# Other places for weights and tokens in SBUF, and another order of three products, in a pool/SSD/ConvFFN layer

## The chip, the core and the metric

The kernel runs on one core of a Trainium2 chip. The metric is the device time of one execution in microseconds, as the median of several runs. Beside it stands one profiled execution, whose trace holds every instruction with its start and length.

The engines of the core appear under these names: PE (TensorE, matrix products), PEld (its loads of weights), DVE (VectorE), ACT (ScalarE), POOL (GpSimd) and SP (SyncE, which here only issues DMAs). SBUF is the on-chip memory of 128 partitions; an address below is a byte offset inside a partition. PSUM holds the sums of matrix products.

## The reference

One layer for two request groups that share the weights: 256 tokens of a new stream and 32 tokens of a running one, so 288 tokens of 2048 numbers, all in float32.

```
proj = rmsnorm(x) @ w_in          # 2048 -> u_pool 1024 | z 2048 | xBC 2560 | dt 32
pool = pool_mixer(u_pool)         # trailing means over 2/4/8/16 tokens, then w_pool
ssd  = ssd_mixer(z, xBC, dt)      # causal conv, Mamba-2 scan, gate, grouped rmsnorm
x    = x + rmsnorm(concat[pool, ssd] @ w_out)      # 3072 -> 2048
up   = causal_dwconv(rmsnorm(x) @ w_up)            # 2048 -> 2 x 5632
x    = x + rmsnorm((silu(gate) * val) @ w_down)    # 5632 -> 2048
```

It also returns new states of the pool, the convolutions and the scan. Nearly all arithmetic lies in four products: w_in, w_out, w_up and w_down.

## The kernel before

**Products in two parts.** A float32 number is split in a high part (rounded to the type float32r, in which a matmul streams) and a low part, what is left of it. A product of weights and tokens is then three matmuls into one PSUM sum: high weights by high tokens (L146), high weights by low tokens (L147), low weights by high tokens (L148). Function `mm3` issues these three. Weights are the stationary operand, 128 x 128, loaded anew for each matmul (as many PEld as PE instructions); tokens are the moving operand, 288 columns. A group of three such matmuls, for 128 rows of K (a K-tile) and 128 output columns, is called a triple below.

**Projections.** Function `project` computes one group of output columns, mostly 256 (two PSUM sums of 128): it goes over K in chunks (`ksplit`), fetches each chunk of weights with one DMA on SP's queue into a raw tile (`fetch_w`), splits it in parts of up to 1024 elements a partition, ACT writing the high weights and DVE the low ones (`split_w`, L140 and L141), and issues the triples: for each part, for each of the two sums, for each of the part's K-tiles. A part is four K-tiles of 256 columns. There are 82 such groups: 19 of w_in, 6 of w_out, 42 of w_up, 15 of w_down (in two halves of K, with w_up's second half between). The last two output tiles of w_down are written out by hand at the end of the kernel (L1268, L1269 and L1291), as are the first chunks of w_in at its start (L364). The pool's products (`pool_group`) use `mm3` too.

**Order.** A scheduler that simulates the program orders the instructions of the engines; `tc.high_priority` brings weight fetches and splits ahead, and `pin` fixes the order of some instructions.

**Places in SBUF.** Tiles come from pools, which lie one behind another in a partition in the order in which they are opened; a tile's size is rounded up to 32 bytes. The order is: `const`, `whi` (high weights), `side1`, `wlo` (low weights), `wraw` (raw weights), `apool` (tokens: xn, mixs, hn, each with high and low halves of 288 numbers, 1152 bytes apart), `bpool`, and then the pools of single stages. Weight and token buffers are multiples of 256 bytes long, and so are a K-tile's rows and, at 512 bytes, the two column blocks of a weight tile. All high weights therefore start at one address modulo 256, all low weights at another, and all high tokens at a third. `side1` holds one tile, `rec`, of 64 bytes, so that low weights stand 64 bytes behind the high weights, modulo 256; the tokens, too, stand 64 bytes behind the high weights. `FC_GAP` gives the activations of the feed-forward stage (fa) the same place as the tokens of `apool`; the pool's outputs in the w_out stage (mixp) stand 128 bytes off it. In the first stage high and low weights are the two halves of one tile, 3072 bytes apart. wlast (the last weights of the tail) lies in raw buffers, which before the change have the tokens' place modulo 256.

Of the kernel before, what the change touches and what calls it, by code (L numbers as in the profile page):

```python
# [8 lines left out]
F32 = mybir.dt.float32  # L9
# [7 lines left out]
P = 128  # L17
# [8 lines left out]
HEADS = 32  # L26
# [3 lines left out]
NX = D_SSD // P  # L30
# [22 lines left out]
TURN_AT = 13  # L53
FC_GAP = 48
NEAR = 8


@with_exitstack
def body(
# [23 lines left out]
    act, dve, pool, pe, sp = nc.scalar, nc.vector, nc.gpsimd, nc.tensor, nc.sync  # L83

    const = ctx.enter_context(tc.tile_pool(name="const", bufs=1))
    wpool = {"hi": ctx.enter_context(tc.tile_pool(name="whi", bufs=4))}
    side1 = ctx.enter_context(tc.tile_pool(name="side1", bufs=1))
    wpool["lo"] = ctx.enter_context(tc.tile_pool(name="wlo", bufs=4))
    wpool["raw"] = ctx.enter_context(tc.tile_pool(name="wraw", bufs=4))
    apool = ctx.enter_context(tc.tile_pool(name="apool", bufs=16))  # L90
    bpool = ctx.enter_context(tc.tile_pool(name="bpool", bufs=20))
    acc_ps = ctx.enter_context(tc.tile_pool(name="acc_ps", bufs=5, space=PSUM))
# [6 lines left out]
    def atile(name):  # L99
        return apool.tile([P, 2, NT], F32R, tag="a", name=name)  # L100

    def btile(name):
        return bpool.tile([P, NT], F32, tag="b", name=name)
# [17 lines left out]
    def fetch_w(view, kb, nk, c0, nc_):  # L121
        raw = wpool["raw"].tile([P, nk, nc_], F32, tag="raw", name="raw")
        with tc.high_priority(offset=ahead[0]):
            group, c = divmod(c0, 2 * P)
            sp.dma_start(out=raw, in_=view[group, :, kb : kb + nk, c : c + nc_])
        return raw

    def split_w(raw, kb, nk, nc_, after=()):

        out = []  # L130
        step = min(nk, 1024 // nc_)
        for k in range(0, nk, step):
            n = min(step, nk - k)
            hi = wpool["hi"].tile([P, n, nc_], F32R, tag="hi", name="whi")
            lo = wpool["lo"].tile([P, n, nc_], F32R, tag="lo", name="wlo")
            with ExitStack() as order:
                order.enter_context(tc.high_priority(offset=ahead[0]))
                for ins in after:
                    order.enter_context(tc.issue_after(ins.ins))
                act.activation(hi, raw[:, k : k + n, :], AF.Copy)  # L140
                dve.tensor_tensor(lo, raw[:, k : k + n, :], hi.bitcast(F32), op=ALU.subtract)  # L141
            out.append([(kb + k + i, hi[:, i, :], lo[:, i, :]) for i in range(n)])
        return out

    def mm3(out, wh, wl, a, start, stop, then=lambda ins: ins):
        then(pe.matmul(out, wh, a[:, 0, :], start=start, stop=False))  # L146
        then(pe.matmul(out, wh, a[:, 1, :], start=False, stop=False))  # L147
        then(pe.matmul(out, wl, a[:, 0, :], start=False, stop=stop))  # L148

    def project(view, groups, acts, ksplit, before=None, done=None, spare=(), hold=(), behind=None, wait=(), tail=()):  # L150


        n_all = sum(-(-w // P) for _, w in groups)
        accs = [acc_ps.tile([P, NT], F32, tag="acc", name="acc") for m in range(n_all - len(spare))]
        accs.extend(spare)
        k_first, k_last = ksplit[0][0], ksplit[-1][0] + ksplit[-1][1] - 1
        after = before(*ksplit[0]) if before else None
        for i, (kb, n) in enumerate(ksplit):
            raws = [fetch_w(view, kb, n, c0, w) for c0, w in groups]
            nxt = None  # L160
            if before and i + 1 < len(ksplit):
                nxt = before(*ksplit[i + 1])
            m0 = 0
            for raw, (c0, w) in zip(raws, groups):
                parts = split_w(raw, kb, n, w, tuple(wait) + ((after or ()) if m0 else ()) + (hold if i else tail if m0 + w // P == n_all else ()))
                for q, part in enumerate(parts):
                    for m in range(w // P):
                        c = slice(m * P, (m + 1) * P)
                        with ExitStack() as order:
                            if behind and part[-1][0] == k_last and m0 + m > SUMS_AFTER:  # L170
                                order.enter_context(tc.issue_after(behind[-1].ins))
                            for k, hi, lo in part:
                                mm3(accs[m0 + m], hi[:, c], lo[:, c], acts[k], k == k_first, k == k_last)
                        if done and i + 1 == len(ksplit) and q + 1 == len(parts):
                            done(m0 + m, accs[m0 + m])
                m0 += w // P
            after = nxt
        return accs
# [14 lines left out]
    start = ExitStack()  # L193
# [35 lines left out]
    first_load(9)  # L229
    cols = const.tile([P, sum(n for _, n in COLS)], F32, name="cols")  # L230
    pin(sp.dma_start(out=cols, in_=cols_in))
    hp = const.tile([HEADS, 3], F32, name="hp")
    pin(sp.dma_start(out=hp, in_=heads_in))
    col = {}
    for name, n in COLS:
# [2 lines left out]

    ones = const.tile([P, P], F32, name="ones")
    pool.memset(ones, 1.0)  # L240
    eps_t = const.tile([P, 1], F32, name="eps_t")
    pool.memset(eps_t, EPS)
    warm = const.tile([P, 1], F32, name="warm")
    pin(act.activation(warm, eps_t, AF.Copy))
# [4 lines left out]
        out=tri, in_=ones, pattern=[[1, P]], compare_op=ALU.is_ge, fill=0.0, base=0, channel_multiplier=-1  # L249
# [79 lines left out]
    for i, (kb, n) in enumerate(CHUNKS):  # L329
# [18 lines left out]
        w = ahead_w.pop(0)  # L348
# [5 lines left out]
        for q, (r, m, k, x) in enumerate(products):  # L354
            if i == len(CHUNKS) - 2 and q == 24:
# [10 lines left out]
                start=kb + k + r + x == 0, stop=kb + k == KD - 1 and r == 1,  # L366
            ))

    for k in range(KD):
        c = slice(HEADS * (k % 4), HEADS * (k % 4 + 1))  # L370
# [6 lines left out]
    pah = const.tile([P, 5 * NXC], F32, name="pah")  # L377
    c0 = 3 * NXC + 3 * KD
    act.activation(pah, cols[:, c0 : c0 + 5 * NXC], AF.Copy, scale=0.5)
    g_ssd = const.tile([P, NX], F32, name="g_ssd")  # L380
    act.activation(g_ssd, col["ssd_norm"], AF.Copy, scale=0.5)
    start.close()

# [83 lines left out]
    with tc.high_priority(offset=EVAC):  # L467
        for i, v in enumerate(v4):
            c = slice(HEADS * i, HEADS * (i + 1))
# [3 lines left out]
    v = v4[0]  # L473

    xs_ps = [project(win, [(O_X, 256)], xn, K16, wait=last_split)]
    xs_in = {}

# [28 lines left out]
    turned = mp.tile([P, 4, MW], F32, tag="m", bufs=2, name="g")[: 3 * HEADS, 0, :]  # L506
# [38 lines left out]
    follow(pe.matmul(p_[:, NX:], ones[:HEADS, :], hv[:, NX:], start=True, stop=True))  # L545
    dve.tensor_copy(tok, p_tok[:, :, : 2 * HEADS].rearrange("p b (r h) -> p b r h", r=2))
    dve.tensor_copy(tokd, p_tok[:, :, 2 * HEADS :])
    wq = const.tile([P, HEADS], F32, name="wq")
    for j in range(3):
        dve.tensor_copy(wq[NS * j : NS * (j + 1)], p_tok[P - NS :, 2, 2 * HEADS :])  # L550
    dcol = const.tile([P, NX + HEADS], F32, name="dcol")
# [4 lines left out]
    for i in range(4):  # L556
        o = btile("bc")
# [103 lines left out]

    def token_rstd(p_, scale, name):

        o = const.tile([P, 3], F32, tag="trs", bufs=2, name=name)
        act.activation(o, p_[:, 0:3], AF.Sqrt, bias=eps_t, scale=scale)
        dve.reciprocal(o, o)
        return o
# [95 lines left out]
    for i in range(1, NX // 2):  # L763
        if XS_RATE[i]:
            ssd_tokens(quads[0])
        ps = project(win, [(O_X + 256 * i, 256)], xn, K16)
        xs_evac(i, ps)
        xs_conv(i - 1)
        run_quads(XS_RATE[i])
# [82 lines left out]
    for t in range(NX):  # L852
        a = atile("mixs")
# [6 lines left out]

    xT = op_.tile([P, NEAR, NT], F32, name="xT2")
    x1 = []
# [45 lines left out]
    for gi in range(2):  # L908
        c = slice(gi * P, (gi + 1) * P)
# [99 lines left out]
    for grp in ((0, 1), (2,), (3,), (4,), (5,), (6, 7)):  # L1009
# [13 lines left out]
        if grp[0] == 0:  # L1023
            sp.dma_start(out=xT.rearrange("p k n -> p (k n)"), in_=x_g[:, KD : KD + NEAR * NT])
            sp.dma_start(out=new_sconv, in_=sc_stage.rearrange("p s r t -> p (s r t)"))
# [36 lines left out]
    for s in range(KD):  # L1062
        pin(dve.tensor_tensor(x1[s], x1[s], rm, op=ALU.mult))
        if s < NEAR:
            pin(dve.tensor_tensor(x1[s], x1[s], xT[:, s, :], op=ALU.add))
        else:
            pin(pool.dma_start(out=x1[s], in_=x_g[:, KD + NT * s : KD + NT * (s + 1)], accum_op=ALU.add))
        while todo and todo[0] + (1 if todo[0] < NEAR else NEAR) <= s:
            hn_of(todo.pop(0))
# [82 lines left out]
    for m in range(0, KD, 2):  # L1152
        for p_ in project(w_down[:, :, 0:HALF, :], [(m * P, 256)], f[:HALF], [(0, 8), (8, 8), (16, 6)]):
            o = btile("part")
# [43 lines left out]
            ))  # L1198

    def factors(src, bias, n, name):  # L1200
        o = const.tile([P, 2], F32, tag="trs", bufs=2, name=name)[:, :n]
        pin(act.activation(o, src, AF.Sqrt, bias=bias, scale=1.0 / D_MODEL))
        pin(dve.reciprocal(o, o))
        return o
# [26 lines left out]
    for (kb, n), raw in zip(K22, raws):  # L1231
        for k in range(0, n, 4):
            m = min(4, n - k)
            if len(parts) < 4:
                hi = wpool["hi"].tile([P, m, 256], F32R, tag="hi", name="whi")
                lo = wpool["lo"].tile([P, m, 256], F32R, tag="lo", name="wlo")
            else:
                rest = wpool["raw"].tile([P, 2, 4, 256], F32R, tag="raw", name="wlast")
                hi, lo = rest[:, 0, :m], rest[:, 1, :m]
# [23 lines left out]
    for n_, part_ in enumerate(parts):  # L1263
        for i, t in enumerate((A, B)):
            for k, hi, lo in part_:
                c, end = slice(i * P, (i + 1) * P), k == HALF - 1
# [50 lines left out]
    for q in range(4):  # L1317
        pin((act if q % 2 else sp).dma_start(
            out=y_sample[0][:, 512 * q : 512 * (q + 1)], in_=xr_s[NS * q : NS * (q + 1), :]
# [8 lines left out]
    p_y = acc_ps.tile([P, 512], F32, tag="acc", name="py_")  # L1328
    pin(pe.matmul(p_y, ident, xr[0], start=True, stop=False))
    rf = factors(sum_0, bias_0, 1, "rf0")  # L1330
    diag = fp.tile([P, P], F32, tag="fc", bufs=6, name="diag")
    pin(act.activation(diag, ident, AF.Copy, scale=rf[:, 0:1]))
# [74 lines left out]
```

## Time and profile before

| | |
|---|---|
| median of 3 runs | 1316.25 us (1314.89 to 1316.63) |
| profiled execution | 1315.22 us |
| its span, first to last instruction | 1313.5 us |
| PE busy | 1306.5 us, 99% |
| DVE busy | 894.9 us, 68% |
| ACT busy | 671.7 us, 51% |
| DMA | 251.75 MB, 192 GB/s in the mean |

A line of the profile names the source line, the engine, the operation, and the tiles it writes and reads, as `acc<-hn,whi` for a matmul of the tokens hn with high weights. A matmul's length is the time that it is in flight, and the next one starts before it ends; how fast PE goes is seen in the distance between two starts. The timeline gives start and length in microseconds from the start of the span.

### The profile page before, as it was taken

Reading aid. Unit: us, or ns where it says so; the run is one execution under the profiler, and the core shown is the slowest. Engines: PE = TensorE matmul, PEld = TensorE weight load, DVE = VectorE, ACT = ScalarE, POOL = GpSimd, SP = SyncE. Lnnn points to the kernel's source line nnn. Section 1 sums busy time; section 2 is a strip of 40 time slices with the busy share of each in tenths; the row PEclk is TensorE's granted clock in tenths of the full one; section 3 lists DMA queues with packets and bytes.
Section 4 is the critical chain, followed back from the end, with each engine's and each line's share of the span. In section 5 each row is a group of like instructions: output and inputs, shape, how many; then the busy total and the mean of one; then the engine's idle time right before and its main releaser. Section 6 shows DMA issues by size and latency. Waiting matters only on the chain.

```text
span 1313.5 us, 25268 instructions
## 1 busy us (share of the span) xinstructions
PE 1306.5 (99%) x10043; PEld 1295.5 (99%) x10043; DVE 894.9 (68%) x1515; ACT 671.7 (51%) x1013; POOL 250.6 (19%) x399
## 2 busy tenths in 40 slices
PE   9999999999999999999999999999999999999998
PEld 9999999999999999999999999999999999999997
DVE  7999988879655588867766743336666666755454
ACT  7558767446543567554544433334444444444442
POOL 2352222212232221211211200001111111201110
PEclk9999999999999999999999999999999999999999
DMA  8578875455666478766545455455544555466663
GB/s 340 189 218 281 284 218 179 157 165 204 205 214 223 140 198 255 210 183 188 184 161 165 159 168 175 155 174 178 176 161 161 174 174 168 161 228 189 212 178 115
DMA packets 110039, 251.75 MB, mean 192 GB/s; under 512 B 64737, under 2 KB 73857, under 8 KB 87393
## 3 DMA queue, kind: packets, MB, share of 16 engines
q1 hardware_dynamic: 103424, 233.22, 54.8%
q0 software_dynamic: 5824, 16.13, 4.2%
q8 instruction: 78, 1.28, 0.4%
q10 hardware_dynamic: 672, 0.80, 0.2%
q14 instruction: 41, 0.33, 0.1%
HBM read 237.11 MB, written 13.00 MB: 190 GB/s over the span
## 4 chain that ended last, share of the span: by engine, by line
PE 94%; DMA 2%; issue 1%; DVE 1%; ACT 0%; POOL 0%; SPq 0%; POOLq 0%; ACTq 0%
PE acc L146 30%; PE acc L147 30%; PE acc L148 29%; DMA raw<-in_w_first 1%; PE py L636 1%; PE acc L1268 0%; DVE w L303 0%; PE acc L1269 0%; DMA mg<-in_x_g 0%; PE acc_t L1291 0%; DVE sq L323 0%; PE py L638 0%; PE acc L364 0%; PE acc_x L364 0%; PE acc_x L146 0%
## 5 line engine op out<-in xcount | busy, mean ns | idle before, releaser
L141 DVE TENSOR_TENSOR wlo<-raw,whi 128x1024 fp32r<-128x1024 f32 (+1 forms) x396 | 473.6, 1198 | 305.9 <-ACT whi L140 304.4
L140 ACT ACTIVATE whi<-raw 128x1024 fp32r<-128x1024 f32 (+1 forms) x396 | 408.1, 1032 | 466.9 <-PE acc L147 370.5
L146 PE MATMUL acc<-hn,whi 128*128 128x288 f32 x1376 | 405.5, 296 | 0.8 <-ACT hn L1044 0.4
L147 PE MATMUL acc<-hn,whi 128*128 128x288 f32 x1376 | 401.9, 293 | 0.0
L148 PE MATMUL acc<-hn,wlo 128*128 128x288 f32 x1376 | 398.1, 290 | 0.0
L146 PEld LDWEIGHTS acc<-hn,whi 128*128 128x128 f32 x1376 | 257.7, 188 | 1.7 <-ACT hn L1044 0.8
L147 PEld LDWEIGHTS acc<-hn,whi 128*128 128x128 f32 x1376 | 258.1, 188 | 0.1
L148 PEld LDWEIGHTS acc<-hn,wlo 128*128 128x128 f32 x1376 | 258.1, 188 | 0.0
L146 PE MATMUL acc<-fa,whi 128*128 128x288 f32 x660 | 195.4, 296 | 0.0
L147 PE MATMUL acc<-fa,whi 128*128 128x288 f32 x660 | 193.4, 293 | 0.0
L148 PE MATMUL acc<-fa,wlo 128*128 128x288 f32 x660 | 191.4, 290 | 0.0
L146 PE MATMUL acc<-xn,whi 128*128 128x288 f32 x608 | 179.3, 295 | 0.0
L147 PE MATMUL acc<-xn,whi 128*128 128x288 f32 x608 | 178.5, 294 | 0.0
L148 PE MATMUL acc<-xn,wlo 128*128 128x288 f32 x608 | 177.5, 292 | 0.0
L146 PEld LDWEIGHTS acc<-fa,whi 128*128 128x128 f32 x660 | 123.9, 188 | 0.0
L147 PEld LDWEIGHTS acc<-fa,whi 128*128 128x128 f32 x660 | 123.9, 188 | 0.0
L148 PEld LDWEIGHTS acc<-fa,wlo 128*128 128x128 f32 x660 | 123.9, 188 | 0.0
L1094 POOL COPY fc_stage<-ebuf 128x4 f32<-128x4 f32 x88 | 26.4, 301 | 473.4 <-DVE ebuf L1093 451.9
L146 PEld LDWEIGHTS acc<-xn,whi 128*128 128x128 f32 x608 | 114.2, 188 | 0.7 <-issue 0.5
L148 PEld LDWEIGHTS acc<-xn,wlo 128*128 128x128 f32 x608 | 114.1, 188 | 0.1
L147 PEld LDWEIGHTS acc<-xn,whi 128*128 128x128 f32 x608 | 114.0, 188 | 0.0
L1089 POOL COPY ebuf<-cols 128x2 f32<-128x2 f32 x88 | 73.0, 830 | 110.0 <-DVE fc L1100 90.6
(338 smaller groups left out, 1797.5 us busy)
## 6 DMA issues: line engine op xcount, KB each, us to landing
raw<-in_w_up SPq DMA_DIRECT2D x80, 1024.0 KB, 5.1
raw<-in_w_in SPq DMA_DIRECT2D x38, 1024.0 KB, 5.2
raw<-in_w_down SPq DMA_DIRECT2D x32, 1024.0 KB, 4.9
raw<-in_w_out SPq DMA_DIRECT2D x24, 1024.0 KB, 5.2
raw<-in_w_down SPq DMA_DIRECT2D x16, 768.0 KB, 4.3
raw<-in_w_up SPq DMA_DIRECT2D x14, 512.0 KB, 4.4
gb<-g_d POOLq DMA_DIRECT2D x8, 832.0 KB, 6.1
raw<-in_w_first SPq DMA_DIRECT2D x5, 768.0 KB, 12.8
```

What stands on the lines that cost most here:

```text
L140: act.activation(hi, raw[:, k : k + n, :], AF.Copy)
L141: dve.tensor_tensor(lo, raw[:, k : k + n, :], hi.bitcast(F32), op=ALU.subtract)
L146: then(pe.matmul(out, wh, a[:, 0, :], start=start, stop=False))
L147: then(pe.matmul(out, wh, a[:, 1, :], start=False, stop=False))
L148: then(pe.matmul(out, wl, a[:, 0, :], start=False, stop=stop))
L636: ins = pe.matmul(y[c, 0:256], xw[:, 0, f_], m[:, h, 0:256], start=True, stop=False)
L1089: pool.tensor_copy(e[:, 258:260], hist_f[:, :, i])
L1094: pool.tensor_copy(fc_stage[:, :, :, i], e[:, 256:324].rearrange("p (s c) -> p s c", c=34)[:, :, 0:2])
```

## The change

Six small tiles change pools. `hp`, `eps_t` and the two buffers of `trs` go from `const` to `side1`, `wq` and `g_ssd` from `const` to a new pool `side2` between the raw weights and the tokens. `const` becomes 320 bytes shorter, `side1` 128 longer, and `side2` has 192. High weights move by 320 bytes, low weights by 192, tokens not at all; modulo 256 the low weights then stand at 192 from the high weights and the tokens at 128.

`mm3` gets a switch `other`, with which the second and third product change places: high by high, low by high, high by low. `project` counts its calls and sets the switch in the first 30 calls and in each eighth after that (32, 40, ... 80: 37 of 82), there only in the first part of the first chunk's first group: four K-tiles by two sums (or eight by one), so eight triples. An argument of `mm3` that nobody used goes.

```diff
+ALWAYS = 30
+RESET_AT = 8
...
     wpool["raw"] = ctx.enter_context(tc.tile_pool(name="wraw", bufs=4))
+    side2 = ctx.enter_context(tc.tile_pool(name="side2", bufs=1))
     apool = ctx.enter_context(tc.tile_pool(name="apool", bufs=16))
...
-    def mm3(out, wh, wl, a, start, stop, then=lambda ins: ins):
-        then(pe.matmul(out, wh, a[:, 0, :], start=start, stop=False))
-        then(pe.matmul(out, wh, a[:, 1, :], start=False, stop=False))
-        then(pe.matmul(out, wl, a[:, 0, :], start=False, stop=stop))
+    def mm3(out, wh, wl, a, start, stop, other=False):
+        pairs = [(wh, 0), (wh, 1), (wl, 0)]
+        if other:
+            pairs[1:] = pairs[:0:-1]
+        for n, (w, x) in enumerate(pairs):
+            pe.matmul(out, w, a[:, x, :], start=start and n == 0, stop=stop and n == 2)
+
+    groups_done = [0]
...
+        groups_done[0] += 1
+        turned = groups_done[0] <= ALWAYS or groups_done[0] % RESET_AT == 0
...
-                                mm3(accs[m0 + m], hi[:, c], lo[:, c], acts[k], k == k_first, k == k_last)
+                                mm3(accs[m0 + m], hi[:, c], lo[:, c], acts[k], k == k_first, k == k_last, turned and i + m0 + q == 0)
...
-    hp = const.tile([HEADS, 3], F32, name="hp")
+    hp = side1.tile([HEADS, 3], F32, name="hp")
...
-    eps_t = const.tile([P, 1], F32, name="eps_t")
+    eps_t = side1.tile([P, 1], F32, name="eps_t")
...
-    g_ssd = const.tile([P, NX], F32, name="g_ssd")
+    g_ssd = side2.tile([P, NX], F32, name="g_ssd")
...
-    wq = const.tile([P, HEADS], F32, name="wq")
+    wq = side2.tile([P, HEADS], F32, name="wq")
...
-        o = const.tile([P, 3], F32, tag="trs", bufs=2, name=name)
+        o = side1.tile([P, 3], F32, tag="trs", bufs=2, name=name)
...
-        o = const.tile([P, 2], F32, tag="trs", bufs=2, name=name)[:, :n]
+        o = side1.tile([P, 2], F32, tag="trs", bufs=2, name=name)[:, :n]
```

## The prediction

> **What bounds the kernel now.** I read the page first: busy shares, then the chain that ended last, then the costliest groups.
>
> ```profile
> span 1313.5 us, 25268 instructions
> PE 1306.5 (99%) x10043; PEld 1295.5 (99%) x10043; DVE 894.9 (68%) x1515; ACT 671.7 (51%) x1013; POOL 250.6 (19%) x399
> ...
> PE 94%; DMA 2%; issue 1%; DVE 1%; ACT 0%; POOL 0%; SPq 0%; POOLq 0%; ACTq 0%
> ...
> L146 PE MATMUL acc<-hn,whi 128*128 128x288 f32 x1376 | 405.5, 296 | 0.8 <-ACT hn L1044 0.4
> ```
>
> PE is on the chain for 94% of the span, nearly all in the three products of a K-tile step (L146 high weights by high tokens, L147 high by low, L148 low by high). The last column of L146 says that it hardly ever waits. PE's waits for weights, of all its waits (total, times, longest):
>
> ```profile
> PE acc L146 <- ACT whi L140: 0.2, 1, 0.2
> ```
>
> So the time is number of matmuls times the distance between their starts. The mean of 296 ns is the time in flight and overlaps the next; the distance comes from the timeline, in order of time (start, length).
>
> ```profile
> 599.98 0.30 PE L146 MATMUL acc<-hn,whi 128*128 128x288 f32 x1
> 600.12 0.29 PE L147 MATMUL acc<-hn,whi 128*128 128x288 f32 x1
> 600.25 0.29 PE L148 MATMUL acc<-hn,wlo 128*128 128x288 f32 x1
> 600.37 0.30 PE L146 MATMUL acc<-hn,whi 128*128 128x288 f32 x1
> ...
> 623.97 0.30 PE L146 MATMUL acc<-hn,whi 128*128 128x288 f32 x1
> ```
>
> Read the first and last: L146 starts at 599.98 and at 623.97, 61 triples later, so a triple takes 393.3 ns. Inside it the three distances are unequal, about 135, 131 and 127.5 ns. The windows say that the rate holds:
>
> ```profile
> 47.00:105.00 58.00, 58.00 (x444) 58.00 (x443) 57.11 (x132) 31.63 (x47) 29.10 (x30) 1.00 0.63 189
> 105.00:310.00 205.00, 205.00 (x1692) 200.80 (x1691) 178.81 (x326) 138.35 (x255) 45.02 (x61) 1.00 0.65 213
> 530.00:1286.00 756.00, 756.00 (x5769) 756.00 (x5768) 458.60 (x741) 343.91 (x456) 104.75 (x171) 1.00 0.55 177
> ```
>
> Columns: stretch; length; busy time (instructions) of PE, weight loads, DVE, ACT, POOL; granted clock; DMA share; GB/s. 5769 matmuls in 756 us are 131.0 ns each, a third of 393.3, at full clock. The instructions of line 148 (count; shortest, median and longest time in flight; first and last start), of eight rows (one for each pair of tiles) the first and the fifth:
>
> ```profile
> L148 PE MATMUL acc<-hn,wlo x1376: 290/290/300, 472.1 to 1165.1; 128*128 128x288 f32 x197
> ...
> L148 PE MATMUL acc<-mixp,wlo x128: 290/290/298, 337.8 to 465.0; 128*128 128x288 f32 x128
> ```
>
> The eight counts add up to 3076 triples, 3076 x 393.3 ns = 1210 us of the 1313.5. The change can only matter through this distance.
>
> **Does the distance depend on the address?** While a product streams its tokens, the weights of the next are loaded (each matmul has its own weight load). Call d the distance in bytes, modulo 256 and in steps of 64, from the tokens being streamed to the weights being loaded. Today high weights, low weights and tokens stand at 0, 64, 64, and the low half of a token tile lies 1152 bytes, so 128, behind the high half. L146 streams high tokens and L147's high weights load: d = 3. L147 streams low tokens (192), low weights load (64): d = 2. L148: d = 3. Elsewhere in the trace the same three products stand otherwise. In the first stage (L364) high and low weights are halves of one tile, 3072 bytes apart, so d = 3, 1, 3. For the mixp tiles, which begin 128 bytes further, d = 1, 0, 1. In the tail the weights in wlast stand where the tokens do: L1269 has d = 0, L1268 (320 columns, half from either token half) 0 and 2. The states' matmuls of 512 columns (L977) have d = 2, the last before L978 d = 0.
>
> ```profile
> 9.21 0.96 PE L364 MATMUL acc_x<-xn,w 128*128 128x288 f32 x6
> ...
> 18.81 0.96 PE L364 MATMUL acc_x<-xn,w 128*128 128x288 f32 x6
> ```
> ```profile
> 363.95 0.30 PE L146 MATMUL acc<-mixp,whi 128*128 128x288 f32 x1
> ...
> 365.92 0.29 PE L146 MATMUL acc<-mixp,whi 128*128 128x288 f32 x1
> ```
> ```profile
> 1296.43 0.31 PE L1268 MATMUL acc<-fa,wlast 128*128 128x320 f32 x1
> ...
> 1298.92 0.31 PE L1268 MATMUL acc<-fa,wlast 128*128 128x320 f32 x1
> ```
> ```profile
> 369.06 0.39 PE L977 MATMUL pst<-xh,bt_h 128*128 128x512 f32 x1
> ...
> 370.22 0.40 PE L977 MATMUL pst<-xh,bt_l 128*128 128x512 f32 x1
> 370.45 0.40 PE L978 MATMUL pst<-xs,bt_s 96*128 96x512 f32 x1
> ```
>
> First stage: 9.60 us for 24 triples, 400.0 ns. mixp: 1.97 us for 5, 394, within rounding 393.3. wlast: 2.49 us for 9 pairs, 276.7 ns. L977: 1.16 us for 5, 232 ns, and about 234 for the one with d = 0 (two decimals are too few there; I take 2.4 ns more). So yes: 400.0 against 393.3 with the same shapes and clock.
>
> **The change part by part.**
>
> *The places.* hp, eps_t, the two trs buffers, wq and g_ssd leave the pool ahead of the weights (rounded up to 32: 32+32+64+128+64 = 320 bytes). 128 of them go between high and low weights, 192 between raw tiles and tokens. Tokens and all behind them stay put. No instruction is added; the six tiles are as large and as far from every engine's path as before: 0. Now high, low, tokens stand at 0, 192, 128, and d becomes 2, 3, 2.
>
> If each d had a price S for 288 columns, whatever came before, the sums above fix them: 2·S3 + S1 = 400.0, 2·S3 + S2 = 393.3, 2·S1 + S0 = 393.3, and a fourth. With wlast for the fourth, (320/288)·(S0+S2)/2 + S0 = 276.7: S0..S3 = 133.9, 129.7, 123.0, 135.2, and the new triple 2·S2 + S3 = 381.2. With the 512-column rows for it, S0 - S2 = 2.4: 128.3, 132.5, 125.9, 133.7, and 385.5. That this is crude shows in the triple itself, whose two d = 3 products stand 135 and 127.5 ns apart. I take the middle, 383.3 ns, 10.0 less than today. It is also near three times 127.5 (382.5), the shortest distance that a product of the triple now keeps up. Ends: 378 (under that shortest distance) and 404 (first rival).
>
> *Where that is worth something.* From 47 to 105 us DVE is busy 57.11 of 58 us: a faster PE would meet it there, so 148 triples (444/3) get nothing. From 105 to 310 DVE has 26 us to spare, later more, and DMA is busy 0.55 to 0.65 of the time. The 128 mixp triples go to d = 0, 1, 0: 397.5 or 389.1, so 0. The tail's 11 us of L1268 to L1291 move by some tenths either way: 0.
>
> *The other order.* In 37 of 82 groups (the first 30, then 32, 40, ... 80) the first eight steps go high·high, low·high, high·low: 296 triples with d = 1, 2, 0. By the sums above S0+S1+S2 = 386.7 in either solution, 6.7 ns less than today. Between the bounds that the tail gives (below, 10.7 ns a pair either way, so 16 a triple) these steps are worth +-4.7 us. Low weights are wanted one product, 0.13 us, sooner in those steps; behind L146 nothing waits for them now (0.2 us in all for weights), so 0, and at most 37 x 0.13 = 4.8 us if DVE's subtraction were late. Low tokens are wanted one product later: nothing.
>
> *Sum.* 3076 - 148 - 128 - 296 = 2504 triples x 10.0 = 25.0 us, plus 296 x 6.7 ns = 2.0: 27.0 us. The profiled execution took 1315.2 us (span 1313.5 and 1.7 around it), 1.0 below the median of 1316.25. 1316.25 - 27 = **1289 us**.
>
> **Rivals.**
>
> *Slower: what is lost is lost per weight load, and d = 2 is dear.* The 512-column rows are the only ones with d = 2 alone. The first matmuls, of 288 columns on constant data, run at about half speed:
>
> ```profile
> 3.62 0.92 PE L270 MATMUL acc_x<-busy 128*128 128x288 f32 x3
> L270 PE MATMUL acc_x<-busy x12: 442/442/607, 1.3 to 4.1; 128*128 128x288 f32 x12
> ```
>
> (Three in 0.92 us from the first start to the last end, each 442 ns in flight, the median: two distances are 478.) The L270 distance is so 239 to 240 ns; half of 240/288 = 0.833 ns a column is an estimate of a column at the full clock without loss: 213.3 ns for 512, so about 18.3 of the 232 are lost. If a 288-column product loses as much, S2 = 138.3, S3 = 127.5 (the very distance behind L148), and the new triple is 404.1: 2504 x 10.8 - 2.0 = +25 us, **1341**. It decides once S2 is above 131.1. Against it: mixp and wlast then need S1 = 145 and S0 = 103, below the 120 that an unhampered product would take. 0.20.
>
> *Slower: the sequence settles in its slower rhythm.* The tail keeps two rates at the same addresses:
>
> ```profile
> 1286.35 0.31 PE L1268 MATMUL acc<-fa,whi 128*128 128x320 f32 x1
> ...
> 1292.36 0.31 PE L1268 MATMUL acc<-fa,whi 128*128 128x320 f32 x1
> ```
> ```profile
> 1294.45 0.31 PE L1268 MATMUL acc<-fa,whi 128*128 128x320 f32 x1
> ...
> 1295.87 0.31 PE L1268 MATMUL acc<-fa,wlast 128*128 128x320 f32 x1
> ```
>
> 22 pairs in 6.01 us, 273.2 ns, and after a pause five in 1.42, 284: 3.9% more. So what came before matters, and the steps in another order may throw the sequence from one rhythm into another, for better or worse. 383.3 x 1.039 = 398.4: 2504 x 5.1 ns - 2 = +11, **1327**. 0.10.
>
> *Nothing.* The 393.3 ns hold for d = 3, 2, 3 and for 1, 0, 1. If that is where most arrangements settle, the time stays at **1316**, within a few us. 0.12.
>
> The Trainium skill's page "TensorE: Matmul & The Clock Gate", Part 2, "Step-by-step: what each phase is for", speaks for it: it gives TensorE two independent SBUF read ports, one for the streamed operand and one for the weight load, so that the load takes nothing from a running matmul. By it addresses are free and the change is worth 0, so 1316. The same page (Part 1, "Wait — 56ns, not 53.3ns?") gives N/2.4 + 2.5 ns between warm matmuls, by which 122.5 ns is an estimate here; this trace has 131.1 and 133.3, and the rows differ with the address alone, so here the measurement goes against the rule.
>
> **How the numbers follow.** Faster 0.58 (its own range 1274 to 1302), nothing 0.12, slower rhythm 0.10, dear d = 2 0.20. A measurement tells about 0.2%, 2.6 us, from no change; so faster 0.58, same 0.12, slower 0.30. The fast end of 378 ns gives 2504 x 15.3 + 2.0 = 40 us, 1276. The range takes in that end with a few us of the other order's bound, no change and the slower rhythm, 1273 to 1330, and leaves out the dearest case.
>
> **What will show it.** Right: the timeline at 600 us has L146 every 383 ns (380 to 387), and some 5900 matmuls (756 us at 127.8 ns) fit where 5769 did; the first stage is still at 400. Wrong: a triple of 393 or more at 600 us; two rates in turn that change at the groups 32, 40, 48, ...; PE waiting for wlo at the first step of a group; or DVE behind PE's waits between 105 and 310 us.

## The result, and the profile after

The changed kernel takes 1310.98 us (median of 5 runs, 1309.46 to 1311.6), the kernel before 1316.25 (5 runs, 1314.69 to 1316.64): a ratio of 0.9961, 95% interval 0.9947 to 0.9976. It is faster by 5.3 us (0.4%) where 27 were forecast.

All three products of a triple now stand on one line, L153 (the first stage is L373, the splits L143 on ACT and L144 on DVE). Span, busy shares and chain, from the page of the changed kernel:

```profile
span 1309.3 us, 25267 instructions
PE 1301.1 (99%) x10043; PEld 1289.8 (99%) x10043; DVE 894.0 (68%) x1515; ACT 671.5 (51%) x1013; POOL 248.2 (19%) x399
...
PE 94%; issue 2%; DMA 2%; ACT 1%; DVE 0%; POOL 0%; ACTq 0%; POOLq 0%
```

PE is the bound as before. The distance of the triples, from its timeline in order of time (start, length; two products with whi that follow each other make one row):

```profile
599.71 0.29 PE L153 MATMUL acc<-hn,wlo 128*128 128x288 f32 x1
599.85 0.42 PE L153 MATMUL acc<-hn,whi 128*128 128x288 f32 x2
600.11 0.29 PE L153 MATMUL acc<-hn,wlo 128*128 128x288 f32 x1
...
623.89 0.29 PE L153 MATMUL acc<-hn,wlo 128*128 128x288 f32 x1
```

From the first to the last wlo product lie 62 triples in 24.18 us, 390.0 ns each, against 393.3 before. In the trace's nanoseconds two kinds alternate: 387 (131, 130, 126) and 393 (131, 130, 132). It's a rhythm with a period of two triples, 780 ns. A rhythm, below, is such a pattern of distances that repeats by itself.

The windows, with the columns of the prediction's (stretch; length; busy time and instructions of PE, weight loads, DVE, ACT, POOL; granted clock; DMA share; GB/s):

```profile
47.00:105.00 58.00, 58.00 (x448) 58.00 (x445) 56.92 (x133) 31.33 (x45) 27.90 (x31) 1.00 0.64 193
105.00:310.00 205.00, 204.15 (x1682) 199.30 (x1681) 176.91 (x322) 137.43 (x254) 49.53 (x59) 1.00 0.65 213
300.00:340.00 40.00, 40.00 (x304) 40.00 (x303) 35.53 (x71) 24.81 (x43) 8.67 (x15) 1.00 0.64 216
530.00:1286.00 756.00, 756.00 (x5810) 756.00 (x5810) 463.49 (x747) 346.88 (x461) 101.34 (x173) 1.00 0.55 177
```

In the long stretch 5810 matmuls fit where 5769 did: 41 x 131.0 ns = 5.4 us, as much as the whole gain. Between 105 and 310 us there are ten fewer than the 1692 of before, and PE stands idle for 0.85 us.

### The profile page after: what moved, and what is told of

It reads as the page before. It is cut to its first block, busy times and chain, and to the rows that moved or that the text cites. A ratio compares the mean times of both kernels' runs of the same rounds, so it can differ in the third digit from the quotient of the medians.

```text
span 1309.3 us, 25267 instructions
## 1 busy us (share of the span) xinstructions
PE 1301.1 (99%) x10043; PEld 1289.8 (99%) x10043; DVE 894.0 (68%) x1515; ACT 671.5 (51%) x1013; POOL 248.2 (19%) x399
## 4 chain that ended last, share of the span: by engine, by line
PE 94%; issue 2%; DMA 2%; ACT 1%; DVE 0%; POOL 0%; ACTq 0%; POOLq 0%
PE acc L153 87%; PE acc L373 2%; PE acc_x L373 1%; PE acc_x L153 1%; DMA gb<-g_d 1%; PE py L645 1%; ACT m L627 1%; PE acc L1277 0%; PE acc L1278 0%; DMA xg<-in_x_g 0%; DMA mg<-in_x_g 0%; DMA g_d<-g 0%; PE py L647 0%; ACT whi L143 0%; PE acc_t L1300 0%
## 5 line engine op out<-in xcount | busy, mean ns | idle before, releaser
L144 DVE TENSOR_TENSOR wlo<-raw,whi 128x1024 fp32r<-128x1024 f32 (+1 forms) x396 | 473.1, 1197 | 298.4 <-ACT whi L143 297.7
L143 ACT ACTIVATE whi<-raw 128x1024 fp32r<-128x1024 f32 (+1 forms) x396 | 408.0, 1032 | 454.6 <-PE acc L153 363.4
L153 PE MATMUL acc<-hn,whi 128*128 128x288 f32 x2752 | 539.1, 294 | 0.5 <-ACT hn L1053 0.4
L153 PEld LDWEIGHTS acc<-hn,whi 128*128 128x128 f32 x2752 | 436.6, 188 | 1.3 <-ACT hn L1053 0.8
L153 PE MATMUL acc<-hn,wlo 128*128 128x288 f32 x1376 | 399.7, 292 | 0.0
L153 PEld LDWEIGHTS acc<-hn,wlo 128*128 128x128 f32 x1376 | 258.9, 188 | 0.0
L153 PE MATMUL acc<-fa,whi 128*128 128x288 f32 x1320 | 257.6, 293 | 0.0
L153 PE MATMUL acc<-xn,whi 128*128 128x288 f32 x1216 | 240.3, 294 | 0.3 <-ACT whi L143 0.3
L153 PEld LDWEIGHTS acc<-fa,whi 128*128 128x128 f32 x1320 | 209.1, 188 | 0.0
L153 PEld LDWEIGHTS acc<-xn,whi 128*128 128x128 f32 x1216 | 193.6, 188 | 1.3 <-ACT whi L143 0.6
L153 PE MATMUL acc<-fa,wlo 128*128 128x288 f32 x660 | 192.1, 291 | 0.0
L153 PE MATMUL acc<-xn,wlo 128*128 128x288 f32 x608 | 177.7, 293 | 0.3 <-DVE wlo L144 0.3
L153 PEld LDWEIGHTS acc<-fa,wlo 128*128 128x128 f32 x660 | 124.3, 188 | 0.0
L153 PEld LDWEIGHTS acc<-xn,wlo 128*128 128x128 f32 x608 | 114.4, 188 | 0.7 <-DVE wlo L144 0.5
L153 PE MATMUL acc<-mixs,whi 128*128 128x288 f32 x512 | 100.8, 294 | 0.0
L1107 ACT ACTIVATE fc<-ebuf,cols 128x290 f32<-128x290 f32 x88 | 54.4, 623 | 76.8 <-DVE ebuf L1102 76.2
L1109 DVE SCALAR_TENSOR_TENSOR fc<-ebuf,cols,fc 128x290 f32<-128x290 f32 x176 | 90.2, 517 | 3.9 <-ACT fc L1107 1.2
L153 PEld LDWEIGHTS acc<-mixs,whi 128*128 128x128 f32 x512 | 81.4, 188 | 0.0
L153 PE MATMUL acc<-mixs,wlo 128*128 128x288 f32 x256 | 74.3, 293 | 0.0
L153 PE MATMUL acc<-mixp,whi 128*128 128x288 f32 x256 | 50.5, 293 | 0.0
```

What stands on the lines that cost most here:

```text
L153: pe.matmul(out, w, a[:, x, :], start=start and n == 0, stop=stop and n == 2)
L1107: act.activation(c, e[:, 0:290], AF.Identity, bias=col["f_b"][:, i : i + 1], scale=f_w[:, 0, i : i + 1])
L1109: dve.scalar_tensor_tensor(c, e[:, r_ : r_ + 290], f_w[:, r_, i : i + 1], c, op0=ALU.mult, op1=ALU.add)
```

## Where the time went, stretch by stretch

Both kernels have 10,043 matmuls, so the n-th can be set against the n-th. The table has how much later (+) or earlier (-) than in the kernel before the matmul comes that there starts at the time in the first column (us, worked out from the starts in the traces; the last three columns are experiments told below; the trace of the order alone is of an execution of 1319.92 us, 2.3 above the median of that kernel).

| time before | changed kernel | places alone, shorter execution | places alone, longer execution | order alone |
|---|---|---|---|---|
| 47 | +0.28 | +0.45 | +1.21 | +0.43 |
| 105 | +0.02 | -0.04 | +0.72 | +0.50 |
| 150 | +2.03 | +0.54 | +1.30 | +3.79 |
| 310 | +1.45 | +1.04 | +1.81 | +4.12 |
| 530 | +1.03 | +0.08 | +2.05 | +3.95 |
| 900 | -1.77 | -3.05 | +11.45 | +4.12 |
| 1286 | -4.77 | -6.32 | +21.27 | +4.25 |

The changed kernel loses 2.0 us between 105 and 150 us and gains 5.8 from 530 to 1286, that is 3.0 ns for each of the 1922 triples there. In the tail behind 1286 us it loses 0.6 again (-4.77 there, -4.2 between the two spans).

The loss has a place. PE's waits of the changed kernel between 119 and 124 us, with the idle time and its releaser in brackets, and ACT's timeline just before:

```profile
119.69 0.40 PE L153 MATMUL acc<-xn,wlo 128*128 128x288 f32 x1 [0.28 <-DVE wlo L144]
123.17 0.80 PE L153 MATMUL acc<-xn,whi 128*128 128x288 f32 x4 [0.34 <-ACT whi L143]
```
```profile
103.63 1.06 ACT L143 ACTIVATE whi<-raw 128x1024 fp32r<-128x1024 f32 x1 [0.83 <-PE acc L153]
108.52 0.31 ACT L595 ACTIVATE ce<-gb 128x128 f32<-128x128 f32 x1 [3.82 <-DMA gb<-g_d]
...
112.40 5.03 ACT L627 ACTIVATE m<-gb,tok 128x256 f32<-128x256 f32 x16
117.33 1.05 ACT L143 ACTIVATE whi<-raw 128x1024 fp32r<-128x1024 f32 x1
```

With the new places but the usual order everywhere (the first experiment), ACT does two splits in the same stretch:

```profile
109.38 1.07 ACT L143 ACTIVATE whi<-raw 128x1024 fp32r<-128x1024 f32 x1 [2.01 <-PE acc L153]
110.35 0.30 ACT L595 ACTIVATE ce<-gb 128x128 f32<-128x128 f32 x1
...
115.97 1.05 ACT L143 ACTIVATE whi<-raw 128x1024 fp32r<-128x1024 f32 x1
```

That is also what the kernel before does (109.41 and 116.00 us). With the other order the scheduler, which simulates the program to order each engine's instructions, puts ACT's wait for a DMA and sixteen operations of the scan (L627) ahead of the next split, and PE finds weights missing. So an edit to PE's order alone moved work on ACT. PE's first wait ends with DVE's split, which had waited for ACT's of 117.33 us, and the second with ACT's next one, of 122.08 us; by the distances of the starts they cost 0.55 and 0.6 us, and what made up the rest of the 2.0 us was not taken apart. The other traces, each set against the kernel before, support ACT's order as the cause: the four with the new one (the changed kernel, and e2, e3 and e6 below) lose 1.2 to 4.2 us between 105 and 150 us, the four with the old one (e1, e4, e5 and e7) 0.0 to 0.6. But e3 loses its 1.2 without a wait of PE for weights that the profile shows.

## The experiments

All kernels that begin with e compute the layer. Those that begin with m hold matmuls alone: they leave out the layer and return zeros, and their time says nothing but the distances. In them all weights and tokens lie in one tile; places are (low weights, tokens) in steps of 64 bytes from the high weights, so (1, 1) is the kernel before, (0, 1) its first stage and (3, 2) the changed kernel. The diffs of e1 to e5 are against the changed kernel, those of e6 and e7 against the kernel before. The experiments ran on three chips; the kernel before took 1315.5 to 1315.9 us on each of them.

### The two parts apart

e1: the new places, no step in the other order.

```diff
-ALWAYS = 30
-RESET_AT = 8
+ALWAYS = 0
+RESET_AT = 1000
```

> The new places with the old order everywhere. Theory A (the places set the distance between matmuls, the other order only costs): a triple of the steady stretch takes 390.0 ns (387 and 393 in turn) as in the changed kernel, the steps in the other order (396.6 ns there) are gone, and the time is 1 to 4 us under the changed kernel's, 1307 to 1310 us. Theory B (the other order brings PE into the faster rhythm, the places alone do not): steady triples of 393.3 ns or more, time 1315 us or more.

e2: the other order, the old places.

```diff
-    hp = side1.tile([HEADS, 3], F32, name="hp")
+    hp = const.tile([HEADS, 3], F32, name="hp")
...
-    wq = side2.tile([P, HEADS], F32, name="wq")
+    wq = const.tile([P, HEADS], F32, name="wq")
...
```

> The old places with the new order in 37 groups. Theory A: normal triples stay at 393.3 ns; the 296 triples in the other order have d = 3, 0, 1 from the old places and cost between -1 and +3 us in all, so 1315 to 1319 us. Theory B: steady triples go to 390 ns and the time to 1311 us.

e1: six executions took 1309.14 and 1335.47 to 1336.57 us (five of them), beside 1315.47 before. One execution fits the time of theory A, five that of theory B. e2: 1317.63, ratio 1.0018 (1.0009 to 1.0027). e1 taken once more, to see the longer case in a trace:

> The new places with the old order once more, for its trace. Theory C: where the execution takes 1336 us, triples between 530 and 1286 us stand 400.0 ns apart (400.0 - 390.0 = 10 ns by 2700 triples is the 27 us between the two times that the same program showed), with PE as busy as ever. Rival: the 27 us lie elsewhere, in waits for weights or in the stage to 530 us.

It took 1336.75. The long stretch of the same program, first of the shorter, then of the longer execution, and the timeline of the longer one:

```profile
530.00:1286.00 756.00, 756.00 (x5814) 756.00 (x5813) 461.98 (x746) 347.03 (x461) 106.94 (x173) 1.00 0.55 177
```
```profile
530.00:1286.00 756.00, 756.00 (x5626) 756.00 (x5625) 448.75 (x730) 337.13 (x447) 104.10 (x169) 1.00 0.54 173
```
```profile
599.77 0.43 PE L153 MATMUL acc<-hn,whi 128*128 128x288 f32 x2
...
623.97 0.43 PE L153 MATMUL acc<-hn,whi 128*128 128x288 f32 x2
```

60 triples in 24.20 us, 403.3 ns where 400.0 were expected, at full clock, with the same addresses and instructions that go at 390.0 in the other execution. Both traces run alike to 500 us, at 390 in some stretches and 399 to 400 in others; at 511 to 513 us one falls into 403.3, the other into 390.0, and each keeps it for 750 us. So the new places don't have one price: they have several rhythms, and something small decides. In e2 a triple takes 393.3 (62 in 24.387 us by the trace's nanoseconds), also after each change of order:

```profile
599.57 0.29 PE L152 MATMUL acc<-hn,wlo 128*128 128x288 f32 x1
...
623.96 0.29 PE L152 MATMUL acc<-hn,wlo 128*128 128x288 f32 x1
```

In the blocks of eight turned triples that nothing else breaks up (25 in each kernel) a turned triple, one in the other order, took 397.6 ns in the mean, and 396.7 in the changed kernel. The other order is no gain of its own.

### Is there a price per distance?

m1 goes through the 16 places in both orders, twice; m2 repeats one product with d from 0 to 7 in steps of 32 bytes.

```python
BLOCKS = [triple(lo, tok, other) * 24 for other in (False, True) for lo in range(4) for tok in range(4)]
BLOCKS += BLOCKS[::-1]
# m2
BLOCKS = [single(d, n, 8) for n in (288, 256, 512) for d in range(8)]
```

> Leaves out the whole computation: matmuls alone, 24 triples each at all 16 places of low weights and tokens (steps of 64 bytes from the high weights), in both orders, and then all of it again from last to first. Theory A: the rate hangs on the places alone: 393.3 ns at (low weights 1, tokens 1), 400 at (0, 1), 390 at (3, 2) in the normal order, the same in both passes; by one price per distance d, 2.S2 + S3 = 390 fixes S2 near 128.9, S3 near 132.2, S1 near 135.6, S0 near 122.1. Theory C (what came before sets the rhythm): the same places give two different rates in the two passes. If places do nothing, all 64 blocks take 393.

> Leaves out the whole computation: one product over and over, weights d times 32 bytes ahead of the tokens (d = 0 to 7), 40 times each, for 288, 256 and 512 columns, and for 288 columns once more with the tokens 32 bytes lower. If each distance has a price of its own, 288 columns show steady distances that differ with d, near S0 = 122, S1 = 136, S2 = 129, S3 = 132 ns at d = 0, 2, 4, 6; if the price is paid per weight load, the loss is the same number of ns at 512 columns as at 288; if addresses do nothing, all d give one distance.

Measured, ns a triple in the usual order (rows: low weights 0 to 3; columns: tokens 0 to 3), and in the other:

```
        usual order                     other order
lo 0    396.7  400.0  393.3  397.8     396.7  400.0  393.3* 396.7
lo 1    398.3  393.3  400.0  393.3     396.7  397.8  400.0  393.3*
lo 2    393.3* 397.8  400.0  396.7     398.3  403.3  400.0  393.4
lo 3    396.7  400.0  400.0  400.0     398.3  393.3  396.7  393.3
* second pass: 400.0 (2, 0), 396.7 (0, 2 other), 400.0 (1, 3 other)
```

Matmuls alone repeat what the kernels show: 393.3 at (1, 1), 400.0 at (0, 1), 396.7 for the other order at (3, 2). But the usual order at (3, 2) went at 400.0, both times, where theory A had 390. From the timeline of m1, the stretches of (1, 1) and (3, 2) (length less the last product's 0.30 us, by the distances: 8.65 us for 66, 8.13 for 61):

```profile
64.30 8.95 PE L98 MATMUL acc<-big 128*128 128x288 f32 x67
150.81 8.43 PE L98 MATMUL acc<-big 128*128 128x288 f32 x62
```

And m2, 288 columns with d = 0 and d = 32 bytes, 512 columns with d = 0 and d = 96 bytes:

```profile
16.94 4.64 PE L95 MATMUL acc<-big 128*128 128x288 f32 x34
22.21 4.70 PE L95 MATMUL acc<-big 128*128 128x288 f32 x34
...
97.79 7.42 PE L95 MATMUL acc<-big 128*128 128x512 f32 x32
125.31 7.90 PE L95 MATMUL acc<-big 128*128 128x512 f32 x33
```

The means of its steady parts, in ns, are 131.7, 133.3, 133.3 and 132.3 for d = 0, 64, 128 and 192 bytes at 288 columns. Added up, 2 S3 + S2 is 397.9 for the old places and 2 S2 + S3 is 398.9 for the new; neither 393.3 nor 390.0 comes out. Prices don't add.

### What leads into which rhythm

m3 tries several entries, that is, products that go ahead of a steady sequence: at the new and the old places, 20 triples in the usual order behind a single product of 32 to 472 columns, or behind 1 to 16 triples in the other order.

```python
BLOCKS += [one(tok, n) + triple(lo, tok, False) * 20, triple(lo, tok, True) * 8 + triple(lo, tok, False) * 20]
```

> Leaves out the whole computation: matmuls alone. At the new places (low weights 3, tokens 2) and at the old ones (1, 1) a single product of 32 to 472 columns, then 20 triples in the normal order, then 8 in the other order and 20 in the normal one; then the same with 1, 2, 4 and 16 in the other order. Theory C (two rhythms at the new places, and the other order leads into the shorter one): behind the single product the normal triples take 400 ns for some or most lengths and 390 for the rest, behind eight in the other order 390 each time, and with one or two of them not always; at the old places 393.3 throughout. Rival D (in matmuls alone only the first block's 400 ns exists; the 390 need the changing addresses of the real tiles): 400 ns everywhere at the new places, whatever goes ahead.

At the new places, behind a single product: 400.0 for 32, 72, 112, 192, 272, 312, 352, 392 and 472 columns, 403.4 for 152, 390.0 for 232 and 432. Behind the other order, 1, 2, 4, 8 or 16 triples of it: 390.0, all 16 times. At the old places: 393.3 to 393.4 behind everything. The rows show three steady rhythms at one set of addresses, behind 112 columns, 152 columns and 8 triples of the other order (6.13 us for 46, 5.51 for 41, 6.36 for 49 distances: 133.3, 134.4, 129.8):

```profile
55.12 6.43 PE L107 MATMUL acc<-big 128*128 128x288 f32 x47
74.77 5.81 PE L107 MATMUL acc<-big 128*128 128x288 f32 x42
65.75 6.66 PE L107 MATMUL acc<-big 128*128 128x288 f32 x50
```

In the kernel, how often is the other order needed? e3 keeps it in the first 30 groups, the last of which begins at 549 us, and drops the later ones:

```diff
-RESET_AT = 8
+RESET_AT = 1000
```

> The changed kernel with the other order in the first 30 groups alone, none after that. Theory C: nothing throws the sequence off in the last 52 groups, as it has no pause there, so triples stay at 390.0 and the seven left-out places save 56 x 6.6 ns and what follows them, 0.4 to 1 us: 1310 us. If single executions fall into the longer rhythm late, some come out 10 to 25 us longer.

It took 1310.41 us (1309.53 to 1312.77), ratio 0.9962 (0.9948 to 0.9975), as the changed kernel. Its long stretch:

```profile
530.00:1286.00 756.00, 756.00 (x5813) 756.00 (x5813) 462.69 (x744) 347.32 (x461) 105.43 (x173) 1.00 0.55 177
```

Once in the 390 rhythm, nothing throws the sequence out: between 530 and 1286 us PE never waits. e5 keeps all 37 groups, but turns one triple in each instead of eight:

```diff
-... turned and i + m0 + q == 0)
+... turned and i + m0 + q + m == 0 and k == k_first)
```

> The changed kernel with one triple in the other order, instead of eight, in the same 37 groups. Theory C: one is enough to lead into the 390 ns, as the matmuls alone showed, so steady triples stay at 390.0 and 259 triples save up to 6.6 ns each, 1 to 1.7 us: 1309 to 1310 us. If eight are needed, single executions fall to 1320 to 1337 us.

The expectation failed: 1324.07 us (1321.7 to 1324.68), ratio 1.0056 (1.0042 to 1.007), slower than before. Four stretches between turned triples:

```profile
580.00:676.00 96.00, 96.00 (x741) 96.00 (x740) 67.88 (x121) 45.84 (x61) 16.86 (x29) 1.00 0.59 181
680.00:919.00 239.00, 239.00 (x1795) 239.00 (x1794) 118.87 (x160) 97.78 (x125) 17.20 (x29) 1.00 0.50 166
925.00:1018.00 93.00, 93.00 (x718) 93.00 (x717) 61.57 (x109) 44.15 (x59) 16.07 (x29) 1.00 0.51 170
1025.00:1242.00 217.00, 217.00 (x1629) 217.00 (x1628) 131.66 (x218) 99.12 (x133) 30.79 (x50) 1.00 0.56 181
```

741 in 96 us are 388.7, 718 in 93 us 388.6, 1795 in 239 us 399.4, 1629 in 217 us 399.6 ns a triple (parts of a matmul at the edges make these some tenths of a per cent too low): one turned triple throws the sequence into 390, into 400, or leaves it. In the trace's nanoseconds it depends on where in its rhythm the sequence is hit. A turned triple that followed one of 136, 126, 139 ns led to 390 (four of four after 520 us), one that followed 133, 134, 132 (or 133) stayed at 400 (three of three), and one that followed the 393 ns half of the 390 rhythm fell to 400 (three of three). One that followed the 387 ns half stayed at 390 (six of six, before 440 us). So in this trace it is not chance but the state in which the sequence is met.

Eight in a row led back to 390 each of the seven times after 560 us in the changed kernel. That alone doesn't show that eight are needed, for each of these seven followed a 387 ns half, where one is enough. Two other groups do, which start at 112.3 to 114.1 and at 517.4 to 519.3 us and are met in the 400 ns rhythm behind a triple of 399 or 400 ns in all three kernels: eight led to 390 in the changed kernel and in e3, four of four; one stayed at 400 in e5, two of two. Eight behind a 393 ns half, with nothing between, occur in no trace.

### Is anything shorter than 390?

m4 runs the 16 places in five orders (usual, other, the two in turn, and two reversed), m5 64 places in steps of 32 bytes with four entries.

```python
# m4
BLOCKS = [six(*products(lo, tok))[kind] * 12 for kind in KINDS for lo in range(4) for tok in range(4)]
# m5, for each place
BLOCKS += [other + normal * 13, one(tok, 112) + normal * 13, one(tok, 232) + normal * 13, (normal + other) * 7]
```

> Leaves out the whole computation: matmuls alone, 16 places by five orders of two triples (normal, other, the two in turn, and each with its second triple from last to first), 24 triples each. Theory C: again sums of 390 to 403 ns a triple and none at 382 or below, as the distance depends on the sequence as a whole. A price for each distance would make the orders that run back, whose d are those of the same triples, come out at the mean of normal and other.

> Leaves out the whole computation: matmuls alone, 64 places of low weights and tokens (steps of 32 bytes), 13 normal triples each behind one triple in the other order, behind a single product of 112 columns and behind one of 232, and 14 triples with the two orders in turn. Theory C: several places have more than one rhythm; the shortest found lie at 386.7 to 390 ns, none at the 381 to 385 of the prediction, and what stands in front decides among them. At (6, 4) in these steps, the new places: 390, 400, 390. If a price per distance held, the sums would be single-valued.

m4: 390.0 to 403.3, with 390.0 only for the two orders in turn at (1, 3). m5: 390.0 at the new places behind one turned triple and behind 232 columns (400.0 behind 112), again in turn at (1, 3), and nowhere else; no steady distance is below 390.0. The reversed orders of m4 speak once more against added prices: they pass through the same d as the usual and the other order together, and at (2, 2) they took 393.3 ns where both of those took 400.0. (1, 3) went at 393.3 in the usual order behind each entry. A kernel was built on it: the kernel before with 128 bytes more ahead of the tokens, and the two orders in turn (e6), and the same places in the usual order (e7).

```diff
+    side2 = ctx.enter_context(tc.tile_pool(name="side2", bufs=1))
     apool = ctx.enter_context(tc.tile_pool(name="apool", bufs=16))
...
+    space = side2.tile([P, 32], F32, name="space")
+    pool.memset(space[:], 0.0)
...
+                                steps[0] += 1
-... k == k_last)
+... k == k_last, IN_TURN and steps[0] % 2 == 0)
```

> The kernel before, with two edits of another kind: the tokens 128 bytes further (low weights at 64 and tokens at 192 bytes from the high weights, modulo 256), and in all projections the usual and the other order in turn, triple by triple. In the run of orders at 16 places, and again in the run of 64 places, this was the one arrangement beside the changed kernel's that went at 390.0 ns, and in the usual order its places gave 393.3 behind every entry, so no slow rhythm was seen there. Theory (the rhythm is set by addresses and order, and a pause only chooses among those that exist): a mean of 390.0 to 391 ns from 530 to 1286 us, and in 300 to 340 us too, where the changed kernel goes at 394.5 to 399; 2800 triples by 2.5 to 3.3 ns is 7 to 9 us less than before, so 1306 to 1309. Rival (what holds for matmuls alone doesn't carry over where groups, pauses and other products come between): stretches of 396 ns and above, 1314 to 1330.

> The same places as the run before it (tokens 128 bytes further), every triple in the usual order. Theory: 393.3 ns as in the kernel before, though d is now 1, 2, 1: 1314.5 to 1317.5. If the places alone gave 390, 1307; additive prices from the trace of before (2 S1 + S2, 382 to 397) leave it open on both sides.

e6 took 1309.27 us (1308.78 to 1310.81), ratio 0.9952 (0.9939 to 0.9966); e7 1315.58, ratio 1.0001 (0.9992 to 1.001). The long stretch of e7, and of e6 with three others, the second of them where it lost time:

```profile
530.00:1286.00 756.00, 756.00 (x5768) 756.00 (x5768) 458.98 (x742) 344.19 (x457) 103.43 (x171) 1.00 0.55 177
```
```profile
105.00:115.00 10.00, 10.00 (x76) 9.86 (x76) 5.84 (x21) 3.19 (x9) 0.86 (x2) 1.00 0.92 337
115.00:125.00 10.00, 8.13 (x48) 7.67 (x47) 6.62 (x14) 10.00 (x26) 3.34 (x8) 0.83 0.51 147
...
300.00:340.00 40.00, 40.00 (x308) 40.00 (x307) 36.68 (x75) 25.75 (x44) 8.72 (x15) 1.00 0.62 209
530.00:1286.00 756.00, 756.00 (x5815) 756.00 (x5814) 463.86 (x749) 348.04 (x463) 108.95 (x173) 1.00 0.55 177
```

The time of e6 is just above the expected 1306 to 1309. The rhythm is 390.0 in the kernel as it was alone, and between 300 and 340 us, where the changed kernel has 304 matmuls, e6 has 308. Set against its own kernel before it gains 6.2 us, the changed kernel 5.3; the intervals overlap, so that one beats the other isn't shown. Between 105 and 150 us e6 fell back by 4.2 us: as in e2 and the changed kernel ACT's splits come late (PE waits of 1.1 us for whi and 0.7 for wlo), and behind those pauses the granted clock fell to 0.83 in the mean of ten microseconds, with most products 240 ns apart from 121.5 to 124.6 us.

## Why the prediction was wrong in size

*The bound* was right: PE at 99%, and in the changed kernel its longest waits for weights are 0.3 us.

*That the distance depends on the address* was right. The Trainium skill's rule against it (page "TensorE: Matmul & The Clock Gate", Part 2, "Step-by-step: what each phase is for": two independent read ports, so a load takes nothing from a running matmul) does not hold for the products here: 512 columns repeated took 226.7 to 234.3 ns by the place of the weights alone. The same page of the Trainium skill gives N/2.4 + 2.5 ns between warm matmuls (Part 1, "Wait — 56ns, not 53.3ns?"), by which 215.8 ns is an estimate for them.

*The step that failed* is "If each d had a price S for 288 columns, whatever came before". It gave 383.3 ns, 10.0 less; measured are 390.0, 3.3 less, in the rhythm that the changed kernel holds, and 400.0 or 403.3 in the others at the same addresses. m2 measured the prices, which add up to neither triple. Two things beside it went wrong with it. The S were fitted from rows that each settle in a rhythm of their own, so they were never prices. And the support "three times 127.5 (382.5), the shortest distance that a product of the triple now keeps up" took a distance inside a rhythm for one that can be kept: distances of 126 do occur, but always with longer ones beside them, and no steady triple in any run was below 390.0.

*Two rates in turn*, changing at groups 32, 40 and so on, were named as a sign of a wrong forecast. The changed kernel shows only a few triples of 395 to 399 ns behind each of these groups; e5 shows the sign in full.

*The other order* was put at 6.7 ns less than today (-2.0 us). It takes 396.7 ns, 3.3 more: 296 x 3.3 ns = +1.0 us, 3.0 from the forecast and within its bounds of 4.7.

*What hides or delays it.* 47 to 105 us: forecast 0, measured -0.26 us. Low weights wanted sooner: forecast 0, at most 4.8 us; PE's one wait for them, 0.3 us at 119.69, is in a triple of the usual order. But with the changed order on ACT 2.0 us went between 105 and 150. That the scheduler would reorder another engine wasn't in the prediction. The tail: forecast 0 within some tenths, measured +0.6 us. mixp: forecast 0, measured 393.1 instead of 393.8 ns in the mean of 126 triples (these lines: 5 triples in 1.97 us):

```profile
364.73 0.30 PE L153 MATMUL acc<-mixp,wlo 128*128 128x288 f32 x1
...
366.70 0.29 PE L153 MATMUL acc<-mixp,wlo 128*128 128x288 f32 x1
```

The first stage stays at 400.0 as forecast (12 triples from the first to the last of these rows, in 4.80 us):

```profile
12.55 0.96 PE L373 MATMUL acc_x<-xn,w 128*128 128x288 f32 x6
...
17.35 0.96 PE L373 MATMUL acc_x<-xn,w 128*128 128x288 f32 x6
```

*The sum again with measured terms:* 2504 triples x 3.3 ns = -8.3 us, +1.0 for the other order, +2.0 between 105 and 150 us: -5.3, beside the -5.3 measured between medians and -4.2 between the two spans. The terms come from the traces of these spans, so -4.2 is what the sum should give, and that it meets the medians is luck. Stretches at 394 to 400 ns, from 310 to 343 us above all, the triples of 395 to 399 with which each return to 390 begins, and the tail are not in this sum.

*The rivals.* "The sequence settles in its slower rhythm" named the right mechanism: what came before decides between rhythms at the same addresses. It was tied to the wrong part. The places bring the slow rhythms (e1: 1336 in five of six executions, +20 us; the rival had 1327), and the steps in the other order, which the rival feared, keep the kernel out of them. "Dear d = 2" fell with additive prices (m2 has 133.3 ns at 128 bytes where this rival had 138.3, and the same 133.3 at 64 bytes, where it needed 145), though e1's time near its 1341 would have looked like it. "Nothing" was nearer the result (5.3 us away) than the forecast (22 us); that the result lies in the range of 1273 to 1330 says little, as the range took in no change and the slower rhythm.

## What to carry to other kernels

When back-to-back matmuls bound a kernel, a few nanoseconds a product hang on where weights and tokens stand to each other (all runs here count that modulo 256 bytes; whether the period is another was not tried); measure whole sequences at the places in question, from several entries, and don't add prices of single products. Where one arrangement holds several rhythms, look at single executions and not only at a median, and prefer an arrangement with one rhythm behind every entry, or lead the sequence in with enough steps of another kind (here eight did it where one didn't). An edit to one engine's order can move another engine's work where a scheduler plans them together: compare the engines' timelines also where nothing was edited.

## What the runs showed of the hardware that was not expected

- The same instructions at the same addresses and full clock go steadily at 390.0, 400.0 or 403.3 ns a triple, for 750 us on end, by what went before them. The old places go at 393.3 to 393.4 behind all 32 entries of m3.
- Most steady distances are multiples of 3.33 ns (390.0, 393.3, 396.7, 400.0, 403.3), 256 columns repeated took 116.6 to 120.1 ns, and 288 columns 131.7 to 133.3, by the place of the weights.
- At the mixp places of the changed kernel (3, 0) m1 measured 396.7, the kernel 393.0; why they differ was not tried. Open too is which small event at about 511 us sends executions of e1 into one rhythm or the other, and what in the chip makes the rhythms.
